# A two-layer hybrid encoder: the first feed-forward block moved into the stage before it, and the edits that go with it

## The chip, the cores and the metric

The program runs on one core of one Trainium2 chip, in one launch. The metric is the device time of an execution in microseconds (us). The engines are TensorE (PE; its weight loads are counted as PEld), VectorE (DVE), ScalarE (ACT), GpSimd (POOL) and SyncE (SP), which here only issues DMAs.

## The reference, cut to what matters

```python
for l in range(2):                      # 1024 prompt + 64 sample tokens, D = 1024
    m = silu(c) @ w_ada[l] + b_ada[l]   # "conditioning": 6 x 1024 numbers for each of 2 sequences
    sh1, sc1, g1, sh2, sc2, g2 = split(m, 6)
    hn = rms_norm(x, norm_mix[l]) * (1 + sc1) + sh1
    o = even_mix(hn) if l == 0 else odd_mix(hn)   # attention + HGRN2 / gated RG-LRU
    x = x + (1 + g1) * o
    hn = rms_norm(x, norm_ffn[l]) * (1 + sc2) + sh2
    x = x + (1 + g2) * ((silu(hn @ ffn_wg[l]) * (hn @ ffn_wu[l])) @ ffn_wd[l])   # D_FF = 2816
y = rms_norm(x, final_norm)
```

All in float32, with products held to about that precision.

## The kernel before, in words

The state x is kept feature by token: eight tiles of 128 partitions by 1088 tokens, of 4.25 KB per partition each. A float32 product is three passes in the faster matmul type: an operand is split into a high part (a cast on ScalarE, L99) and a low part (a subtraction on VectorE or GpSimd, L100), and TensorE adds hi·hi, hi·lo and lo·hi. `load_w` (L105) fetches a weight of 512 KB by one DMA and splits it; `project` (L304) multiplies loaded weights by split operands into the six banks of "t", "z" and "mm", and VectorE adds each result into x (L317).

**Order of the work.** The text fixes what is computed, and a list scheduler with a simulated timeline sets each engine's order; `soon()` and `later()` raise or lower the priority of what is written in them, and DMAs stand in SyncE's queue in the order so found. The wrappers of L60 and L61 (`oPE`, `oV`, `oS`, `oG`, `oD`) keep an instruction behind everything that the text has before it on that engine.

**Before a feed-forward stage.** The last two output projections of the attention stage (`out_group(3)`, L1091) or of the recurrent stage (`odd_out((6, 7))`, L1297) run over four token chunks of 272, in the order of CH4 (L28). After each chunk, `enter`'s `after` (L336) copies the chunk of x to DRAM ("parks" it, eight DMAs), forms its norm, and builds the operands:

```python
rs = norm_stats(CH4[ci], x, stat_tmp)
```

`norm_stats` (L250) squares the eight tiles (six on ScalarE, two on GpSimd), adds them (VectorE, two of the adds on GpSimd), sums over partitions with matmuls against ones (`rms_sum`, L216), takes the power -1/2 on GpSimd (L233) and spreads the roots by matmuls (`rms_spread`, L236). Then come, for each of eight tiles, a VectorE scaling (L351, in place), a ScalarE high part (L352) and a VectorE low part (L353). Each of these has two pieces in the chunk that holds the border between prompt and sample.

**Up stage** (`up_half`, L357). The 22 column blocks of 128 hidden features are worked as 2 "plain" blocks (gate and up product over the four chunks, L416 to L443) and 20 blocks of seven products in Strassen's manner, on four accumulators X, Y, Z, W of two banks each (L498 on). Between plain block 0 and plain block 1, `sums` (L392) turns the scaled x into the operand combinations T1 to T4: VectorE subtracts, T2 and T3 get their low parts there, T1 and T4 on GpSimd:

```python
split(b, T1[k][:, 0, :], T1[k][:, 1, :], G)
split(c, T4[k][:, 0, :], T4[k][:, 1, :], G)
```

The pool of the up stage has these places: wg and wu (raw weights) two each, wh and wl (split weights) six each, two hidden tiles. Phases share SBUF addresses: a tile of a new phase waits for the last use of the tiles that lay there. A block's hidden tile is written to DRAM, as one DMA in a plain block (L442) and as two halves in the others (L481, L487).

**Down stage** (`down_half`, L510). The hidden blocks come back in groups of 2, 3, 3, 3, 3, 3, 3 and 2. `fetch` loads hid (L522) and the down weights, and splits both. `got = fetch(0)` and `unpark` (24 DMAs that bring the parked x back, L505) stand ahead of the first group.

**Conditioning of layer 1.** It is made in layer 0's down stage from 48 rows of 512 KB; an item is a DMA and two passes, both on VectorE, or one of them on GpSimd and ScalarE (`mods_dve`, L189). `ada_tick` (L1115) is called after each chunk of a group and issues up to three items with lowered priority.

## Time and profile before

| | us |
|---|---|
| median of 3 runs (lowest, highest) | 2880.85 (2873.72, 2883.93) |
| the profiled execution | 2879.69 |
| its span, first to last instruction | 2877.9 |

In the span TensorE is busy for 92%, its weight loads for 89%, VectorE 63%, ScalarE 35% and GpSimd 42%. The DMAs move 260.94 MB, 91 GB/s on average. In the lines below, L312 is line 312 of the kernel, `out<-in` are the program's tile names, "x6" counts instructions, and a bracket at the end of a line of a timeline holds the idle time before it and what ended that. "granted clock" or PEclk is the share of TensorE's full clock in a stretch. `SPq` is SyncE's queue of DMA issues.

### The profile page before, as it was taken

The numbers are of one execution on the slowest core, as the hardware profiler recorded it, in microseconds if no ns is written. First come the engines' busy times: TensorE is split into PE (matmuls) and PEld (weight loads), VectorE is DVE, ScalarE is ACT, GpSimd is POOL, SyncE is SP. The second block draws the span as 40 slices with busy tenths as digits, with TensorE's granted clock in tenths as the row PEclk, the third lists the DMA queues.
The fourth block names the chain that finished last, engine by engine and source line by source line (L and its number), as shares of the span: only waits on it lengthen the run. The fifth ranks groups of instructions, "written<-read, shape, count | busy, mean of one in ns | idle before, by whom it ended". The sixth has DMA issues, their size and how long they took to land. (4 is left out here: it accounts for less than half of the span.)

```text
span 2877.9 us, 44436 instructions
## 1 busy us (share of the span) xinstructions
PE 2643.8 (92%) x17680; PEld 2566.8 (89%) x17680; DVE 1813.5 (63%) x2806; ACT 1012.4 (35%) x1839; POOL 1221.1 (42%) x861
## 2 busy tenths in 40 slices
PE   6998999999896999999799959998789999999998
PEld 6898989998786999999799959998789999989997
DVE  8768664568997344444788774658853444446555
ACT  3224343353545222222322255563342222222112
POOL 6446443355635444444344463444344444423222
PEclk9999988999997999999899979999899999999999
DMA  6232112112212222223644411211212222144211
GB/s 234 90 117 82 54 45 83 40 61 106 73 64 79 68 75 80 72 69 135 214 157 169 130 63 56 73 65 54 92 45 83 69 82 76 68 144 154 96 48 63
DMA packets 103984, 260.94 MB, mean 91 GB/s; under 512 B 17120, under 2 KB 42720, under 8 KB 103776
## 3 DMA queue, kind: packets, MB, share of 16 engines
q1 hardware_dynamic: 103776, 258.10, 26.9%
q8 instruction: 139, 2.28, 0.3%
q14 instruction: 69, 0.57, 0.1%
HBM read 207.36 MB, written 50.69 MB: 90 GB/s over the span
## 5 line engine op out<-in xcount | busy, mean ns | idle before, releaser
L100 POOL TENSOR_TENSOR w_lo<-w_raw,w_hi 128x1024 fp32r<-128x1024 f32 x88 | 237.9, 2712 | 382.6 <-ACT w_hi L99 312.2
L100 POOL TENSOR_TENSOR wl<-wg,wh 128x512 fp32r<-128x512 f32 x168 | 220.0, 1311 | 323.3 <-ACT wh L99 316.8
L449 PE MATMUL accW<-op,wh 128*128 128x272 f32 x1280 | 259.1, 290 | 12.4 <-DVE hid L473 7.5
L449 PE MATMUL accZ<-op,wh 128*128 128x272 f32 x1280 | 248.3, 290 | 10.0 <-ACT wh L99 9.9
L449 PE MATMUL accX<-op,wh 128*128 128x272 f32 x1280 | 245.0, 288 | 0.0
L99 ACT CAST wh<-wg 128x512 fp32r<-128x512 f32 x168 | 103.9, 621 | 397.9 <-PE accX L449 114.9
L128 PE MATMUL ps_mm<-h_hi,w_hi 128*128 128x384 f32 (+1 forms) x640 | 219.6, 343 | 11.1 <-ACT w_hi L99 9.7
L449 PEld LDWEIGHTS accW<-op,wh 128*128 128x128 f32 x1280 | 207.8, 191 | 14.2 <-DVE hid L473 6.1
L128 PE MATMUL ps_mm<-h_hi,w_lo 128*128 128x384 f32 (+1 forms) x640 | 217.9, 342 | 1.9 <-POOL w_lo L100 1.9
L128 PE MATMUL ps_mm<-h_lo,w_hi 128*128 128x384 f32 (+1 forms) x640 | 218.2, 341 | 0.0
L449 PEld LDWEIGHTS accZ<-op,wh 128*128 128x128 f32 x1280 | 200.3, 188 | 17.1 <-ACT wh L99 17.1
L449 PEld LDWEIGHTS accX<-op,wh 128*128 128x128 f32 x1280 | 200.4, 188 | 0.5 <-ACT wh L99 0.5
L449 PE MATMUL accX<-op,wl 128*128 128x272 f32 x640 | 187.4, 293 | 1.0 <-POOL wl L100 1.0
L449 PE MATMUL accW<-op,wl 128*128 128x272 f32 x640 | 186.0, 291 | 0.0
L449 PE MATMUL accZ<-op,wl 128*128 128x272 f32 x640 | 184.2, 288 | 0.0
L317 DVE SCALAR_TENSOR_TENSOR x<-ps_mm,mods,x 128x384 f32<-128x384 f32 (+4 forms) x334 | 151.5, 478 | 50.6 <-PE ps_mm L312 50.1
L99 ACT CAST w_hi<-w_raw 128x1024 fp32r<-128x1024 f32 x86 | 88.7, 1049 | 236.5 <-PE ps_mm L312 154.7
L128 PEld LDWEIGHTS ps_mm<-h_hi,w_hi 128*128 128x128 f32 x640 | 126.0, 197 | 14.3 <-ACT w_hi L99 10.5
L467 DVE TENSOR_TENSOR tg<-accY,tg 128x544 f32<-128x544 f32 x40 | 29.0, 724 | 173.1 <-PE accY L449 173.1
L100 POOL TENSOR_TENSOR wl<-wu,wh 128x512 fp32r<-128x512 f32 x88 | 116.5, 1325 | 45.1 <-ACT wh L99 45.1
L317 DVE SCALAR_TENSOR_TENSOR x<-ps_t,mods,x 128x384 f32<-128x384 f32 (+3 forms) x220 | 106.8, 502 | 43.2 <-PE ps_t L312 43.0
L479 DVE TENSOR_TENSOR hid<-accZ,tg 128x544 f32<-128x544 f32 x40 | 29.0, 724 | 166.4 <-PE accZ L449 166.4
(484 smaller groups left out, 8235.7 us busy)
## 6 DMA issues: line engine op xcount, KB each, us to landing
ada_raw<-in_adaT SPq DMA_DIRECT2D x48, 512.0 KB, 3.6
wg<-in_wg SPq DMA_DIRECT2D x44, 512.0 KB, 3.6
wu<-in_wu SPq DMA_DIRECT2D x44, 512.0 KB, 3.6
w_raw<-in_wd SPq DMA_DIRECT2D x44, 512.0 KB, 4.1
hid_dram<-hid SPq DMA_DIRECT2D x80, 272.0 KB, 2.1
hid_lo<-hid_dram SPq DMA_DIRECT2D x40, 544.0 KB, 5.4
w_raw<-in_w_in_even SPq DMA_DIRECT2D x28, 512.0 KB, 3.7
w_raw<-in_adaT SPq DMA_DIRECT2D x24, 512.0 KB, 3.6
```

The source lines that it names most:

```text
L99: S.copy(hi, src)
L100: (lo_eng or G).tensor_sub(lo, src, hi.bitcast(F32))
L128: PE.matmul(ps[:, :n], a[:, k * P:(k + 1) * P], b[:, c0:c0 + n], start=(i == 0), stop=(i == last))
L317: V.scalar_tensor_tensor(x[m][:, r0:r0 + rn], ps[:, r0 - c0:r0 - c0 + rn], gate[:, m, b:b + 1], x[m][:, r0:r0 + rn], ALU.mult, ALU.add)
L449: PE.matmul(acc[:, j, :Q], a[:, k * P:(k + 1) * P], op[k][:, b, c], start=(start == 1 and i == 0), stop=(i == 11), skip_group_check=True)
L467: V.tensor_sub(t, y_, t)
L479: V.tensor_add(hA, z_, t)
```

## The change

The first plain block of each layer leaves the up stage. `first_block` is written in the stage before, behind its last projection, with its weights loaded and split there, and its matmuls and those of the norms of chunks 2 and 3 go through `oPE`: chunk 0's products, then the norm of chunk 2, chunk 1's products, the norm of chunk 3, and the products of chunks 2 and 3. The norm has all its squares on ScalarE and all adds on VectorE. The parked x is one DRAM tensor, brought back by eight DMAs. T1 and T4 get their low parts on VectorE. The conditioning becomes a class: rows of parts 0 to 2 are worked in layer 0's up stage (two per block), parts 3 and 4 in its down stage (one per turn), part 5 in layer 1's up stage. For its two tables "cbc" the up stage has one wu place instead of two and five wh and wl places instead of six. The first two hidden tiles of a down stage are fetched by `prefetch` two blocks before the end of the up stage, into unit tiles; the first down weights and the parked x are loaded through `oD`.

```diff
@@ -105,7 +105,8 @@
     def load_w(src, pool=None, tag="w", raw=None, S=S, lo_eng=None, bufs=2):
         pool = pool or stage["w"]
         raw = raw or raw_tile()
-        dma(raw, src)
+        if src is not None:
+            dma(raw, src)
...
+    def inv_rms(parts, n, scale_, PE=PE):
+        return rms_inv(rms_sum(parts, n, PE), n, scale_, PE=PE)
+    def norm_stats(chunk, x, tmp, PE=PE, pool=(1, 2)):
         c0, n = chunk
...
             S.activation(a, x[2 * e][:, c0:c0 + n], AF.Square)
-            if e in (1, 2):
+            if e in pool:
                 G.tensor_mul(b, x[2 * e + 1][:, c0:c0 + n], x[2 * e + 1][:, c0:c0 + n])
             else:
                 S.activation(b, x[2 * e + 1][:, c0:c0 + n], AF.Square)
             V.tensor_add(a, a, b)
             if e:
-                (G if e in (1, 2) else V).tensor_add(a, a, acc)
+                (G if e in pool else V).tensor_add(a, a, acc)
             acc = a
-        return inv_rms([lambda: acc], n, 1.0 / 1024)
+        return inv_rms([lambda: acc], n, 1.0 / 1024, PE)
 
...
@@ -333,14 +334,14 @@
 
...
-        def after(ci):
+        def chunk(ci, PE=PE):
             c0, n = CH4[ci]
             r = slice(c0, c0 + n)
             if not B:
                 B.extend([halves(u(t, F32R, "op")) for _ in range(4)] for t in (tag, tag, "C", "C"))
             for k in range(KD):
-                dma(x_dram[k][:, r], x[k][:, r])
-            rs = norm_stats(CH4[ci], x, stat_tmp)
+                dma(x_dram[:, k, r], x[k][:, r])
+            rs = norm_stats(CH4[ci], x, stat_tmp, PE, ())
             o = c0 % HT
             for k in range(KD):
...
-        return (B, x), after
-
-    def up_half(l, plain, t_tag, op_tag):
-        (B12, B11, B21, B22), x = plain
+        def after(ci):
+            if ci < 2:
+                chunk(ci)
+
+        return B, chunk, after
+    def plain_chunk(ci, ws, B, hid, gate, up, PE):
+        c0 = CH4[ci][0]
+        c = slice(c0 % HT, c0 % HT + Q)
+        for acc, w2_ in ((gate, ws[:2]), (up, ws[2:])):
+            i = 0
+            for w, op in zip(w2_, ((B[1], B[2]), (B[0], B[3]))[ci % 2]):
+                for k in range(4):
+                    for a, b in ((w[0], 0), (w[0], 1), (w[1], 0)):
+                        PE.matmul(acc, a[:, k * P:(k + 1) * P], op[k][:, b, c], start=(i == 0), stop=(i == 23))
+                        i += 1
+        h = hid[:, c0:c0 + Q]
+        with soon():
+            S.activation(h, gate, AF.Silu)
+            V.tensor_mul(h, h, up)
+    def first_block(l, plain, w_gate, w_up, hid):
+        B, chunk, _ = plain
+        ws = [(hi[:, o:o + 512], lo[:, o:o + 512]) for hi, lo in (w_gate, w_up) for o in (0, 512)]
+        for ci, tag in enumerate(("z", "t", "mm", "z")):
+            plain_chunk(ci, ws, B, hid, bank(tag)[:, :Q], bank(tag)[:, :Q], oPE)
+            if ci < 2:
+                chunk(ci + 2, oPE)
+        dma(hid_dram[0], hid)
+
+    class Ada:
+        def __init__(self, todo):
+            self.todo = [(i, j) for i in todo for j in range(KD)]
+
+        def open(self, pool, raw, junk):
+            self.raw, self.junk = raw, junk
+            self.cb = load_cbc([pool.tile([P, 1024], F32, name="cbc", tag="cbc", bufs=2) for v in range(2)],
+                               junk(F32))
+
+        def some(self, n):
+            with later():
+                for _ in range(min(n, len(self.todo))):
+                    i, j = self.todo.pop(0)
+                    raw = self.raw()
+                    dma(raw, I["adaT"][48 + i * KD + j])
+                    mods_dve(1, i * KD + j, self.cb, raw, lambda: self.junk(BF16), j % 2 == 0)
+                    if j == KD - 1:
+                        finish_mods(1, i)
+
+    def up_half(l, plain, x, t_tag, op_tag, ada, prefetch):
+        B = B12, B11, B21, B22 = plain[0]
         with phase_pool(f"up{l}") as fp:
-            layout(fp, ("t4", NT, 4), ("t1", NT, 4), ("t3", NT, 4), ("wg", 1024, 2), ("wu", 1024, 2), ("s1", 512, 1),
-                   ("wh", 512, 6), ("wl", 512, 6), ("hid0", NT, 2))
+            layout(fp, ("t4", NT, 4), ("t1", NT, 4), ("t3", NT, 4), ("wg", 1024, 2), ("wu", 1024, 1), ("s1", 512, 1),
+                   ("wh", 512, 5), ("wl", 512, 5), ("cbc", 1024, 2), ("hid0", NT, 2))
+            hid0 = lambda: fp.tile([P, NT], F32, name="hid0", tag="hid0", bufs=2)
 
             def w_split(src):
-                hi = fp.tile([P, 512], F32R, name="wh", tag="wh", bufs=6)
-                lo = fp.tile([P, 512], F32R, name="wl", tag="wl", bufs=6)
+                hi = fp.tile([P, 512], F32R, name="wh", tag="wh", bufs=5)
+                lo = fp.tile([P, 512], F32R, name="wl", tag="wl", bufs=5)
...
             def fetch(f):
                 wg = fp.tile([P, 1024], F32, name="wg", tag="wg", bufs=2)
-                wu = fp.tile([P, 1024], F32, name="wu", tag="wu", bufs=2)
+                wu = fp.tile([P, 1024], F32, name="wu", tag="wu", bufs=1)
                 dma(wg, I["wg"][l, f])
                 dma(wu, I["wu"][l, f])
                 return wg[:, :512], wg[:, 512:], wu[:, :512], wu[:, 512:]
...
                     split(d, T3[k][:, 0, :], T3[k][:, 1, :], V)
-                    split(b, T1[k][:, 0, :], T1[k][:, 1, :], G)
-                    split(c, T4[k][:, 0, :], T4[k][:, 1, :], G)
+                    split(b, T1[k][:, 0, :], T1[k][:, 1, :], V)
+                    split(c, T4[k][:, 0, :], T4[k][:, 1, :], V)
...
                 def plain_block(f, order):
-                    hid = fp.tile([P, NT], F32, name="hid0", tag="hid0", bufs=2)
+                    hid = hid0()
                     with soon():
                         ws = [w_split(w) for w in fetch(f)]
                     for n, ci in zip("XYZW", order):
                         acc = new_acc(n)
...
-                        h = hid[:, c0:c0 + Q]
-                        with soon():
-                            S.activation(h, acc[:, 0, :Q], AF.Silu)
-                            V.tensor_mul(h, h, acc[:, 1, :Q])
+                        plain_chunk(ci, ws, B, hid, acc[:, 0, :Q], acc[:, 1, :Q], PE)
                     dma(hid_dram[f], hid)
...
-                plain_block(0, range(4))
                 ops = sums()
                 plain_block(1, (1, 3, 0, 2))
+                if ada:
+                    with later():
+                        ada.open(fp, lambda: hid0()[:, :1024], lambda dt: u(t_tag, dt, "junk")[:, :1024])
                 for f in range(2, FF):
+                    if f == FF - 2:
+                        got = prefetch()
                     X, Y, Z, W = (new_acc(n) for n in "XYZW")
...
+                    if ada and 2 < f < FF - 3:
+                        ada.some(2)
...
+        return got
 
     def unpark(tag):
         x = [u(tag, name="x") for _ in range(KD)]
-        for c0, n in CH:
-            for k in range(KD):
-                dma(x[k][:, c0:c0 + n], x_dram[k][:, c0:c0 + n])
+        for k in range(KD):
+            oD(x[k], x_dram[:, k, :])
         return x
...
-    def down_half(l, fp, x_tag, t_tag, use):
+    def fetch_hid(f, hi, lo):
+        dma(lo.bitcast(F32), hid_dram[f])
+        with soon():
+            split(lo.bitcast(F32), hi, lo, V)
+        return hi, lo
+
+    def hid_units(f, tag):
+        return fetch_hid(f, u(tag, F32R, "hid_hi"), u(tag, F32R, "hid_lo"))
+
+    def down_half(l, fp, x_tag, t_tag, got, use):
         first = [sum(GROUPS[:gi]) for gi in range(len(GROUPS))]
+        last_group = len(GROUPS) - 1
+        w0 = []
+        for f in range(GROUPS[0]):
+            raw = raw_tile()
+            oD(raw, I["wd"][l, f])
+            w0.append(load_w(None, fp, "wd", raw, bufs=6))
+        x = unpark(x_tag)
         def fetch(gi):
             hs, ws = [], []
             for f in range(first[gi], first[gi] + GROUPS[gi]):
-                if gi == len(GROUPS) - 1:
+                if gi == last_group:
                     t = fp.tile([P, 2, NT], F32R, name="hid", tag="hid", bufs=2)
-                    hi, lo = t[:, 0, :], t[:, 1, :]
+                    hs.append(fetch_hid(f, t[:, 0, :], t[:, 1, :]))
                 else:
-                    tag = t_tag if f < 2 or f % 2 else "C"
-                    hi, lo = u(tag, F32R, "hid_hi"), u(tag, F32R, "hid_lo")
-                dma(lo.bitcast(F32), hid_dram[f])
-                with soon():
-                    split(lo.bitcast(F32), hi, lo, V)
-                hs.append((hi, lo))
+                    hs.append(hid_units(f, t_tag if f % 2 else "C"))
                 ws.append(load_w(I["wd"][l, f], fp, "wd", bufs=6))
             return ws, hs
-        got = fetch(0)
-        x = unpark(x_tag)
         tick, after, last = use(x)
         for gi in range(len(GROUPS)):
-            ws, hs = got if gi == 0 else fetch(gi)
-            if gi == len(GROUPS) - 1 and last:
+            ws, hs = fetch(gi) if gi else (w0, got)
...
-    x_dram = [dram.tile([P, NT], F32, name=f"x_dram{k}") for k in range(KD)]
+    x_dram = dram.tile([P, KD, NT], F32, name="x_dram")
...
-        plain, after = enter(0, x, "A", slots(mp, "kv", 3, 2, 4))
-        out_group(3, after, CH4)
+        plain = enter(0, x, "A", slots(mp, "kv", 3, 2, 4))
+        om = lambda nm: mp.tile([P, 1024], F32R, name=nm, tag="om", bufs=2)
+        be = lambda nm: mp.tile([P, 1024], F32R, name=nm, tag="be", bufs=6)
+        w_first = []
+        for wt, hi, lo in (("wg", om, om), ("wu", be, be)):
+            raw = raw_tile()
+            dma(raw, I[wt][0, 0])
+            w_first.append((hi("w_hi"), lo("w_lo")))
+            split(raw, *w_first[-1])
+        out_group(3, plain[2], CH4)
+        first_block(0, plain, *w_first, mp.tile([P, NT], F32, name="hid0", tag="wt", bufs=2))
...
-    up_half(0, plain, "B", "A")
+    first_hid = lambda tag: lambda: [hid_units(f, tag) for f in range(GROUPS[0])]
+    got = up_half(0, plain, x, "B", "A", Ada((0, 1, 2)), first_hid("B"))
...
-                      fp.tile([P, 1024], F32, name="cbs", tag="ada_raw", bufs=2))
-        todo = [(i, j) for i in range(6) for j in range(KD)]
-
...
+        ada = Ada((3, 4))
         box2 = []
 
         def use(x):
             with later():
+                raw = lambda: fp.tile([P, 1024], F32, name="ada_raw", tag="ada_raw", bufs=2)
+                ada.open(fp, raw, lambda dt: raw() if dt == F32 else fp.tile([P, 1024], BF16, name="junk", tag="junk"))
...
-            return ada_tick, after, None
-
...
+            return lambda ci: ada.some(1), after, None
...
-        plain, after = enter(1, x, "B", slots(gp, "un", 12, 2, 4, Q))
+        plain = enter(1, x, "B", slots(gp, "un", 12, 2, 4, Q))
...
-        odd_out((6, 7), "un", after, CH4)
+        w_first = [load_w(I[wt][1, 0]) for wt in ("wg", "wu")]
+        odd_out((6, 7), "un", plain[2], CH4)
+        first_block(1, plain, *w_first, un_("hid0"))
...
-    up_half(1, plain, "A", "B")
+    got = up_half(1, plain, x, "A", "B", Ada((5,)), first_hid("A"))
...
-        down_half(1, fp, "B", "A", lambda x: (None, None, lambda ws, hs: finish(ws, hs, x)))
+        down_half(1, fp, "B", "A", got, lambda x: (None, None, lambda ws, hs: finish(ws, hs, x)))
```

## Rows read from the trace of the kernel before

**Rows 1.** The page's busy times of the engines, with shares and instruction counts.
```profile
PE 2643.8 (92%) x17680; PEld 2566.8 (89%) x17680; DVE 1813.5 (63%) x2806; ACT 1012.4 (35%) x1839; POOL 1221.1 (42%) x861
```

**Rows 2.** TensorE's waits, whole span: us in total, times, longest us.
```profile
PE ps_o L240 <- POOL r L233: 19.1, 9, 4.8
...
PE ps_t L312 <- ACT w_hi L99: 16.1, 3, 10.6
...
PE accX L435 <- POOL wl L100: 12.1, 2, 6.1
PE accX L435 <- ACT wh L99: 10.8, 2, 5.5
PE accZ L449 <- ACT wh L99: 9.9, 30, 0.3
...
PE accW L449 <- DVE hid L473: 7.5, 4, 3.7
...
PE accW L449 <- DVE tg L484: 4.9, 4, 2.4
```

**Rows 3.** Stretches: us, busy PE PEld DVE ACT POOL, PEclk, DMA share, GB/s.
```profile
865.00:883.00 18.00, 7.03 (x32) 6.54 (x31) 15.43 (x39) 7.68 (x18) 8.53 (x7) 0.50 0.44 155
883.00:907.00 24.00, 24.00 (x186) 24.00 (x186) 22.06 (x49) 18.78 (x39) 6.75 (x6) 0.95 0.22 67
907.00:940.00 33.00, 21.49 (x157) 20.94 (x156) 14.72 (x21) 12.60 (x25) 22.60 (x13) 0.84 0.10 34
960.00:1360.00 400.00, 394.44 (x3099) 388.44 (x3098) 182.18 (x201) 110.03 (x184) 168.73 (x131) 1.00 0.24 81
1360.00:1420.00 60.00, 41.78 (x245) 39.81 (x245) 35.98 (x41) 22.04 (x23) 14.92 (x6) 0.83 0.62 226
1420.00:1640.00 220.00, 213.19 (x1268) 209.98 (x1267) 182.19 (x316) 58.45 (x79) 110.13 (x43) 0.99 0.49 160
1640.00:1720.00 80.00, 49.46 (x272) 45.96 (x272) 65.88 (x136) 36.62 (x80) 48.91 (x40) 0.77 0.20 67
```

**Rows 4.** TensorE in order of time before layer 0's first block (start, us, work).
```profile
871.59 1.44 PE L224 MATMUL ps_o<-ones,ntmp 128*128 128x1 f32 x6 [5.44 <-DVE ntmp L262]
...
881.27 1.65 PE L240 MATMUL ps_o<-ident,r 128*128 128x128 f32 x6 [3.56 <-POOL r L233]
```

**Rows 5.** VectorE in order of time around the same block.
```profile
866.39 2.55 DVE L353 SCALAR_TENSOR_TENSOR op<-x,mods,op 128x272 fp32r<-128x272 f32 x6
...
870.28 0.90 DVE L353 SCALAR_TENSOR_TENSOR op<-x,mods,op 128x272 fp32r<-128x272 f32 x2
...
880.02 8.53 DVE L353 SCALAR_TENSOR_TENSOR op<-x,mods,op 128x272 fp32r<-128x272 f32 x8
...
907.10 0.72 DVE L100 TENSOR_TENSOR op<-x,op 128x544 fp32r<-128x544 f32 x1
```

**Rows 6.** GpSimd in order of time behind that block (operand splits).
```profile
906.95 15.07 POOL L100 TENSOR_TENSOR op<-x,op 128x544 fp32r<-128x544 f32 x7 [17.25 <-ACT op L99]
...
923.19 1.34 POOL L100 TENSOR_TENSOR op<-x,op 128x544 fp32r<-128x544 f32 x1
```

**Rows 7.** SyncE's DMA queue ahead of that block.
```profile
836.20 34.51 SPq L342 DMA_DIRECT2D x_dram<-x  x32
```

**Rows 8.** SyncE's DMA queue at both down starts, TensorE at the second.
```profile
1349.04 7.43 SPq L505 DMA_DIRECT2D x<-x_dram  x14
...
2589.42 0.86 SPq L108 DMA_DIRECT2D w_raw<-in_wd  x2
...
2592.33 0.32 SPq L487 DMA_DIRECT2D hid_dram<-hid  x1
...
2595.09 0.54 PE L312 MATMUL ps_t<-hid_hi,w_hi 128*128 128x384 f32 x1 [4.99 <-ACT w_hi L99]
```

**Rows 9.** Conditioning passes (tile junk) behind down stage 0: us, DVE, ACT busy, DMA.
```profile
1640.00:1690.00 50.00, 13.32 (x22) 5.72 (x10) 0.94 0.33 107
```

More of the change, by code (lines that the diff above doesn't have):

```diff
@@ L244, in rms_inv @@
         return rms_spread(rms_pow(ps, n, scale_, V, G), n, PE)
-    def inv_rms(parts, n, scale_):
-        return rms_inv(rms_sum(parts, n), n, scale_)
-    def norm_stats(chunk, x, tmp):
+    def inv_rms(parts, n, scale_, PE=PE):
+        return rms_inv(rms_sum(parts, n, PE), n, scale_, PE=PE)
+    def norm_stats(chunk, x, tmp, PE=PE, pool=(1, 2)):
         c0, n = chunk
@@ L1110, in hybrid_encoder @@
         ntmp = lambda: fp.tile([P, 384], F32, name="ntmp", tag="ntmp", bufs=7)
-        cb = load_cbc([fp.tile([P, 1024], F32, name="cbc", tag="cbc", bufs=2) for v in range(2)],
-                      fp.tile([P, 1024], F32, name="cbs", tag="ada_raw", bufs=2))
-        todo = [(i, j) for i in range(6) for j in range(KD)]
-        def ada_tick(ci):
-            with later():
-                for n in range(3):
-                    if not todo:
-                        return
-                    i, j = todo.pop(0)
-                    raw = fp.tile([P, 1024], F32, name="ada_raw", tag="ada_raw", bufs=2)
-                    dma(raw, I["adaT"][48 + i * KD + j])
-                    mods_dve(1, i * KD + j, cb, raw,
-                             lambda: fp.tile([P, 1024], BF16, name="junk", tag="junk"), j % 3 != 0)
-                    if j == KD - 1:
-                        finish_mods(1, i)
+        ada = Ada((3, 4))
         box2 = []
@@ L1134, in use @@
             box2.append(box)
-            return ada_tick, after, None
-        x = down_half(0, fp, "A", "B", use)
-        assert not todo
+            return lambda ci: ada.some(1), after, None
+        x = down_half(0, fp, "A", "B", got, use)
+        assert not ada.todo
     h = box2[0][0]
```

15 lines of the change are left out of this document (2 added, 13 removed).

## The prediction

> **What bounds the kernel now.** I read the busy times first, then what TensorE waits for, then the stretches between stages, and last the queues of the other engines around those stretches. TensorE is busy for 2643.8 of 2877.9 us [rows 1], so the other 234 us are the most that any edit outside its own work can win. The list of its waits [rows 2] puts the large ones at the seams: the inverse roots of the norm (19.1 us in nine), the weights of the plain block (12.1 and 10.8 us, two waits each, one per layer), the first down weights (16.1 us, the longest 10.6). The table of stretches [rows 3] gives the size of each: TensorE is busy for 7.0 of the 18 us before the first block, 21.5 of 33 after it, 41.8 of 60 at the first down start, 213.2 of 220 in that down stage and 49.5 of 80 in the norm behind it. Layer 1 repeats layer 0's seam with the same waits (the pairs of [rows 2]).
>
> **First block inside the preceding stage.** Today TensorE ends the output projection at 866.2 (871.6 less 5.4 of idle), waits for the sums of chunk 2, its roots, and the roots of chunk 3, and begins the block at about 882.6, when the last spread is through [rows 4]. The stretch from 883 to 907 is its four chunks [rows 3], 24 us without a gap, 6 each. The change puts chunk 0 at once behind the projection. But the kept order then reads: chunk 0, sum and spread for chunk 2, chunk 1, sum and spread for chunk 3, chunk 2, chunk 3; nothing can slip between a sum and its spread, which lie some 2 us apart because of the power on GpSimd (19.1 us in nine waits [rows 2]). VectorE decides the rest. It finishes chunk 1's operands at 871.2 [rows 5] and is busy for 15.4 of the 18 us of that stretch [rows 3]; eight adds of the statistics now come to it from GpSimd, 0.43 us each by the 272-column operations there (2.55 us for six), 3.4 us. So: chunk 0 from 866.2 to 872.2; sum at 875.0, spread out at 879.8; chunk 1 to 885.8; sum, 2 us, spread out at 890.6; chunk 2 to 896.6. Chunk 3's operands need 32 short VectorE operations, about 0.27 us each for 272 columns in two pieces (half of 0.43, with some overhead), 8 us behind the spread that frees them, so until about 898; the gate half of chunk 3 ends there, the up half 3 us later, some 902. Today it ends at 907: gain 4.5 us. Ends: without any wait 4 x 6 us end at 890, gain 17; with chunks 0 and 1 at the half clock that rows show after today's gap (granted clock 0.50 in that stretch [rows 3]) they take 12 us more, a loss of 5 to 7. One more thing helps: chunk 2's eight operand passes took 8.53 us while GpSimd split the first weights, against 2.55 for six elsewhere [rows 5]; these splits are now done before.
>
> **The weights of block 1.** Their wait, 5.4 and 6.05 us per layer [rows 2], has two causes in the queues. The loads stood behind 32 parked x copies on the DMA queue, until 870.7 [rows 7], and the last two weights' low parts stood behind seven operand splits on GpSimd, 15.07 us [rows 6]. Both go: T1 and T4 split on VectorE costs it 8 x 0.72 = 5.8 us per layer [rows 5], and all four weights of block 1 find free slots since block 0 keeps its own elsewhere. In layer 0 something new is late: by the tile widths in the code the wg buffers of the up stage lie on the two "wt" slots, and the block's hid0 is now in one of them. A wg load then waits for the last chunk's product and its write, which I estimate at 3 us, and from issue to first use a weight takes 5.7 us at the second down start [rows 8]: some 8.7 us in all. The up halves of block 1, 12 us, can cover that if they are issued first. I take 4 us uncovered (ends 0 and 11.4), so a gain of 7.5 in layer 0; in layer 1, where the hidden tile is in "un" and the buffers are free, 10. Both seams together: 2 x 4.5 + 7.5 + 10 = 26.5 us.
>
> A rule of the Trainium skill speaks against splitting on VectorE: SBUF — State Buffer, section "Who interferes with whom", says that a VectorE instruction with two SBUF inputs and a GpSimd one that reads SBUF exclude each other, and the second waits for the whole of the first. The rows agree in one direction: a split on GpSimd beside the sums took 15.07 / 7 = 2.15 us, alone 1.34 [rows 6], while VectorE's stayed at 0.72 [rows 5]; in the other they show it too, chunk 2's passes at 1.07. By the rule block 1's four low parts take 0.8 us more each beside the longer sums, 3.4 us if uncovered, and the seams' sum would be some 23 instead of 26.5.
>
> **Conditioning in three stages.** Of 48 items 16 stay in down stage 0, one per turn instead of three; 24 go to up stage 0 (two per block), 8 to up stage 1. An item costs VectorE one or two passes, and a pass 1.21 us (13.32 us for eleven, each with its accumulator read [rows 9]). These eleven still run between 1640 and 1690, where it has 65.9 of 80 us to do and TensorE idles 30.5 [rows 3], and they make the evictions late before it (6.8 us idle in the down stage). With a third of the work at a third of the pace they end in time. I take 5 of 6.8 and 7 of 13.3: 12 us (ends 0 and 20). In the up stages 36 and 12 passes, 58 us of VectorE, lie beside products; it is busy there for 182 of 400 us [rows 3]. They cost nothing while the accumulators are read in time; if each pass stood in front of one such read, 58 us. The DMA waits of these passes hold VectorE's queue, with the accumulators' readers behind them. I take 4.
>
> **Down stage.** Today the first down weights are issued at 2589.4, before the last hidden half is written at 2592.3, and TensorE starts at 2595.1, 5.7 after the issue [rows 8]. The new loads are kept behind everything on SP's queue that the text has before them, the last hidden write included: issue 2592.7, start 2598.4. That is 8.3 us after the last product (2590.1) where layer 1 now waits 5.0; layer 0 waits 10.6 since the cast stands behind other work, and gains 2.2. Net a loss of 1.1. The eight x loads (4.46 MB) now follow those weights, where today they are issued 30 us early [rows 8]; at the 226 GB/s seen at 0.62 busy [rows 3] all arrive 20 us later or sooner, about when TensorE has filled its six banks and gone round; I take 2 us per layer (ends 0 and 10). What leaves VectorE's queue are the first two hidden splits, in front of the reads of W in the last block, which cost 7.5 + 4.9 us [rows 2]; I take back 4. Sum: a loss of 1.
>
> **Rings.** wh and wl get five slots instead of six, wu one buffer instead of two. Today each block waits 0.33 us for a cast (9.9 in 30 [rows 2]). The next wu can be loaded only after the last split of the present one. Ends: the 9.9 gone, or 1.5 us per block; I take nothing, nearest to that row.
>
> **Sum.** -26.5 - 12 + 4 + 1 = -33.5 from the profiled execution's own 2879.7 (span 2877.9, 1.8 outside it): 2846. The median shown, 2880.85, is 1.2 higher; I say 2847.
>
> **Rivals.**
> Seams held by VectorE: the same operand passes in the same queue, chunk 3 no earlier, layer 0's weights late by all 8.7 us. For it: VectorE busy 15.4 of 18 there. Against: 5 us of collision gone. Only 5 to 10 us of the 26.5 remain: 2866.
> Down start: the pinned loads delay x by 10 us per layer and nothing comes back in the last block: 16 + 4 more, 2867. For it: the x loads stand early today without any cost; against: six banks of slack.
> Slower: the ring of five. In the block loop a product's weight must be released, cast and split before its next use; with one slot fewer each block waits once more, a cast and a split, 0.6 + 1.3 us less the present slack of some 0.4: 1.5 us in each of 40 blocks, 60 us: 2906. From 0.85 us per block on it eats the whole gain. For it: each block already waits for a cast; against: TensorE's order is chosen with the ring known.
> More gain: weights covered wholly, the norm gaining all 20, the last block's waits gone: 2826.
> That the change does not do what it says: the order is kept only on TensorE; if VectorE's queue puts chunk 2's statistics late, chunk 1 waits too; that is the first rival's time.
>
> **How the numbers follow.** Forecast 0.47 (own range 2834 to 2862), VectorE's seams 0.18, down start 0.13, the ring 0.15, more gain 0.07. The range 2824 to 2888 leaves out the ring at full price and the tail of the last case. A measurement of this kernel tells 0.3%, 8.6 us, from nothing. Faster: 0.46 + 0.13 + 0.05 + 0.07 = 0.71; same: 0.01 + 0.04 + 0.06 = 0.11; slower: 0.15 + 0.01 + 0.02 = 0.18.
>
> **What would show it.** Right: the idle before the first block gone and instead two gaps of 2 us or more between sum and spread among its chunks; block 1's wait under 4 us; no conditioning pass in the last down group; first down product some 8 us after the last up product in both layers. Wrong: TensorE idle per block above 0.33 us in the block loop, waits for hid or x at the down start above 5 us, or chunk 2 and 3 starting when they do today.

## The result: slower by 1.1%

The changed kernel takes 2913.3 us (median of 4; 2908.7 to 2917.6) against 2881.7 for the kernel before, a ratio of 1.0114 with a 95% interval of 1.0089 to 1.014. The forecast was 2847, with a range of 2824 to 2888. The profiled executions are 2908.7 us (span 2906.9) and 2879.7 (2877.9).

The page's busy times after:

```profile
PE 2653.2 (91%) x17680; PEld 2570.7 (88%) x17680; DVE 1860.4 (64%) x2854; ACT 1018.5 (35%) x1847; POOL 1206.3 (41%) x803
```

TensorE does the same 17680 matmuls; its idle time grew from 234 us [rows 1] to 254, and its busy time by 9. Where the 29 us of span lie is seen by cutting both spans at the same points, read from the first and last matmuls of each stage. "18 blocks" are the last 18 of the 20 seven-product blocks.

| stretch, us | before | after | difference |
|---|---|---|---|
| start to the end of the attention stage's projection | 866.2 | 865.0 | -1.2 |
| to the 18 blocks, layer 0 (both plain blocks, sums) | 121.3 | 118.7 | -2.6 |
| 18 blocks, layer 0 | 400.9 | 447.9 | +47.0 |
| down stage 0 and norm, to the recurrent stage's first product | 327.6 | 305.5 | -22.1 |
| recurrent stage, to its projection's end | 353.1 | 346.7 | -6.4 |
| to the 18 blocks, layer 1 | 121.4 | 123.3 | +1.9 |
| 18 blocks, layer 1 | 399.6 | 412.3 | +12.7 |
| rest | 287.8 | 287.6 | -0.2 |

The loss is in the two up stages, 59.7 us. TensorE's waits over the span (us in total, times, longest), to be held against [rows 2]:

```profile
PE accW L487 <- DVE hid L515: 34.3, 16, 2.3
PE accX L370 <- ACT wh L99: 25.4, 2, 12.8
...
PE accX L487 <- ACT wh L99: 11.9, 30, 0.7
...
PE ps_t L313 <- ACT w_hi L99: 10.5, 3, 5.0
...
PE accX L370 <- POOL wl L100: 9.0, 2, 5.6
```

The first line has grown from 7.5 us in 4 waits [rows 2]: now the products on W waited 16 times for VectorE's read of W (L515, L473 before). Fourteen of these waits, of 2.32 us each, stand among the 16 blocks with conditioning (12 blocks in layer 0, 4 in layer 1); the other two, of 0.91 us, stand in the last block of each layer. From one block's first product on Y to the next one's it takes 25.1 to 27.3 us with conditioning and 22.0 without (21.8 before). The second line says that the wait for block 1's weights did not go; it doubled.

One block with conditioning on VectorE, in order of time (start, us, work):

```profile
1012.97 0.72 DVE L512 TENSOR_TENSOR hid<-accZ,tg 128x544 f32<-128x544 f32 x1 [3.11 <-PE accZ L487]
1013.61 2.34 DVE L196 SCALAR_TENSOR_TENSOR junk<-hid,cbc 128x1024 bf16<-128x1024 f32 x1
...
1015.88 0.71 DVE L526 TENSOR_TENSOR tg<-accW,tg 128x544 f32<-128x544 f32 x1
1016.51 1.13 DVE L441 SCALAR_TENSOR_TENSOR wg<-wg 128x512 f32<-128x512 f32 x1
1017.57 2.92 DVE L528 TENSOR_TENSOR hid<-hid,tg 128x544 f32<-128x544 f32 x1
1020.41 2.31 DVE L196 SCALAR_TENSOR_TENSOR junk<-hid,cbc 128x1024 bf16<-128x1024 f32 x1
...
1022.66 2.30 DVE L196 SCALAR_TENSOR_TENSOR junk<-hid,cbc 128x1024 bf16<-128x1024 f32 x1
...
1025.49 0.71 DVE L515 TENSOR_TENSOR hid<-accW,hid 128x544 f32<-128x544 f32 x1
...
1035.77 0.72 DVE L509 TENSOR_TENSOR tg<-accY,tg 128x544 f32<-128x544 f32 x1 [6.78 <-PE accY L487]
```

and on GpSimd and TensorE in the same block:

```profile
1014.83 2.27 POOL L100 TENSOR_TENSOR wl<-wu,wh 128x512 fp32r<-128x512 f32 x1
1017.06 2.85 POOL L193 TENSOR_TENSOR hid<-hid,cbc 128x1024 f32<-128x1024 f32 x1
1019.87 4.01 POOL L100 TENSOR_TENSOR wl<-wg,wh 128x512 fp32r<-128x512 f32 x2
```

```profile
1026.26 0.52 PE L487 MATMUL accW<-op,wh 128*128 128x272 f32 x2 [2.32 <-DVE hid L515]
```

Three passes of the conditioning and an operation that lasts 2.92 instead of 0.72 us stand between VectorE's read of Z and its read of W. A little later VectorE is idle for 6.8 us. TensorE loses 2.32 us, and then runs slowly. Two stretches of TensorE (columns as in [rows 3]), just behind this wait and after it:

```profile
1026.20:1030.20 4.00, 3.94 (x19) 3.94 (x20) 2.65 (x5) 0.62 (x1) 1.75 (x1) 0.58 0.44 154
1030.20:1040.00 9.80, 9.60 (x77) 9.38 (x75) 1.14 (x2) 2.24 (x4) 2.58 (x2) 1.00 0.05 18
```

A granted clock of 0.58 for 4.0 us (near the lower of the two levels, 1.2 of 2.4 GHz) costs 1.7 us more. Wait and clock together are 4.0 us here; the mean loss over the 16 blocks is 59.7 / 16 = 3.7. The clock did not fall each time: it fell behind ten of the fourteen waits, and in layer 0 a block with such a fall mostly takes 26.6 us and one without 25.1. By these numbers the fourteen waits (32.5 us) and ten falls (some 17) explain about 50 of the 59.7 us; the other 10 were not followed line by line.

The seam in layer 0 (a seam is the stretch from the projection's end to the 18 blocks), TensorE and SyncE's queue; instructions that go through the wrappers carry the wrappers' line, L51:

```profile
873.53 0.94 PE L51 MATMUL ps_o<-ident,r 128*128 128x128 f32 x6 [1.32 <-POOL r L234]
882.57 0.93 PE L51 MATMUL ps_o<-ident,r 128*128 128x128 f32 x6 [1.49 <-POOL r L234]
...
909.60 0.82 PE L370 MATMUL accX<-op,wh 128*128 128x272 f32 x2 [12.61 <-ACT wh L99]
915.15 0.59 PE L370 MATMUL accX<-op,wl 128*128 128x272 f32 x1 [3.36 <-POOL wl L100]
```

```profile
901.93 0.32 SPq L386 DMA_DIRECT2D hid_dram<-hid  x1
904.75 0.33 SPq L425 DMA_DIRECT2D wg<-in_wg  x1
```

The first block runs as meant, right behind the projection, and ends at 897.0 instead of 907.9. Block 1 then waits 12.6 us for the casts of its weights and 3.4 for a low part: their loads were issued at 904.75, behind the write of the first block's hidden tile. In layer 1 the waits are 12.8 and 5.6 us; there the loads follow the write at once (issued at 2125.72), and the casts of these weights, at 2131.20, come right behind the sums' casts on ScalarE. The wait for a low part has a third cause, in VectorE and GpSimd:

```profile
906.27 7.70 DVE L100 TENSOR_TENSOR op<-x,op 128x544 fp32r<-128x544 f32 x12
```

```profile
909.63 6.70 POOL L100 TENSOR_TENSOR wl<-wg,wh 128x512 fp32r<-128x512 f32 x2 [27.12 <-ACT wh L99]
```

The first of these two low parts took 5.46 us, the second 1.28. The first ended 1.1 us behind the last of VectorE's twelve splits in a row (913.97), of which eight are those of T1 and T4 that the change had moved there. In layer 1 it took 7.73 us.

### The profile page after: what moved, and what is told of

Its sections match the earlier page's. It is cut to its first block, busy times and chain, and to the rows that moved or that the text cites. A ratio compares the mean times of both kernels' runs of the same rounds, so it can differ in the third digit from the quotient of the medians.

```text
span 2906.9 us, 44480 instructions
## 1 busy us (share of the span) xinstructions
PE 2653.2 (91%) x17680; PEld 2570.7 (88%) x17680; DVE 1860.4 (64%) x2854; ACT 1018.5 (35%) x1847; POOL 1206.3 (41%) x803
## 5 line engine op out<-in xcount | busy, mean ns | idle before, releaser
L100 POOL TENSOR_TENSOR wl<-wg,wh 128x512 fp32r<-128x512 f32 x164 | 259.1, 1581 | 365.8 <-ACT wh L99 365.3
L487 PE MATMUL accW<-op,wh 128*128 128x272 f32 x1280 | 266.1, 294 | 41.5 <-DVE hid L515 34.3
L487 PE MATMUL accX<-op,wh 128*128 128x272 f32 x1280 | 257.2, 297 | 13.2 <-ACT wh L99 11.9
L487 PEld LDWEIGHTS accX<-op,wh 128*128 128x128 f32 x1280 | 208.1, 196 | 20.6 <-ACT wh L99 19.2
L100 POOL TENSOR_TENSOR wl<-wu,wh 128x512 fp32r<-128x512 f32 x84 | 125.2, 1491 | 107.7 <-ACT wh L99 107.7
L487 PEld LDWEIGHTS accX<-op,wl 128*128 128x128 f32 x640 | 125.7, 196 | 7.5 <-POOL wl L100 7.5
```

The lines of the kernel that those rows point to most:

```text
L100: (lo_eng or G).tensor_sub(lo, src, hi.bitcast(F32))
L487: PE.matmul(acc[:, j, :Q], a[:, k * P:(k + 1) * P], op[k][:, b, c], start=(start == 1 and i == 0), stop=(i == 11), skip_group_check=True)
```

## The experiments

Times are medians beside runs of the kernel before on the same chip; its medians there were 2878.3 (e1_back to e4_before_cond), 2879.7 (n1_vonly, s1_gq, s3_first, s4_t_pool) and 2881.4 (p1_placed_pool, b1_before_placed, s5_more). Between these groups the ratios compare better than the times.

| run | us | ratio to before (95%) | 18 blocks, layers 0 and 1 | down 0 and norm | seams, layers 0 and 1 |
|---|---|---|---|---|---|
| e1_back | 2870.8 | 0.998 (0.997 to 0.999) | 401.2, 399.7 | 326.0 | 120.7, 120.7 |
| e2_back_rings | 2876.8 | 1.000 (0.999 to 1.001) | 403.5, 400.3 | 329.1 | 118.2, 118.2 |
| e3_placed | 2852.8 | 0.992 (0.990 to 0.994) | 399.8, 399.6 | 307.4 | 118.1, 121.8 |
| e4_before_cond | 2915.6 | 1.014 (1.012 to 1.016) | 448.8, 412.3 | 301.7 | 125.3, 122.4 |
| n1_vonly | 2883.5 | 1.002 (1.001 to 1.003) | 420.7, 405.6 | 309.7 | 118.1, 123.2 |
| p1_placed_pool | 2852.7 | 0.990 (0.989 to 0.992) | 395.4, 397.7 | 309.1 | 119.2, 122.1 |
| b1_before_placed | 2862.0 | 0.994 (0.992 to 0.995) | 404.0, 400.1 | 299.8 | 124.4, 121.6 |
| s1_gq | 2856.7 | 0.993 (0.991 to 0.994) | 399.6, 401.2 | 306.2 | 118.5, 123.2 |
| s3_first | 2835.8 | 0.985 (0.983 to 0.987) | 400.6, 398.8 | 306.2 | 110.7, 112.7 |
| s4_t_pool | 2839.1 | 0.986 (0.984 to 0.988) | 401.2, 400.3 | 305.7 | 111.1, 111.0 |
| s5_more | 2829.6 | 0.982 (0.981 to 0.984) | 400.5, 398.7 | 301.4 | 106.9, 112.8 |

The stretches are from one profiled execution each. The first stretch (863 to 871 us among them) shows that a stretch of one execution can't be read closer than a few us.

### Is it the conditioning or the ring? (e1_back, e2_back_rings, e4_before_cond)

```diff
-    got = up_half(0, plain, x, "B", "A", Ada((0, 1, 2)), first_hid("B"))
+    got = up_half(0, plain, x, "B", "A", None, first_hid("B"))
-        ada = Ada((3, 4))
+        ada = Ada(range(6))
-            return lambda ci: ada.some(1), after, None
+            return lambda ci: ada.some(3), after, None
-    got = up_half(1, plain, x, "A", "B", Ada((5,)), first_hid("A"))
+    got = up_half(1, plain, x, "A", "B", None, first_hid("A"))
```

> The changed kernel with all 48 conditioning items back in down stage 0, three per turn; the rest, the ring of five included, as changed. Theory (the passes in the up stages stand in front of the reads of accumulator W): the 16 blocks that take 26.3 us instead of 22.0 lose 4.3 each, 69 us; the down stage takes back some 16 of the 22 us that it had gained: 2913 - 69 + 16 = 2860. Rival (the ring of five slots and the single wu buffer make the blocks slow): the blocks stay at 26, and the down stage gets slower: 2929.

Measured 2870.8, 43 us below the change: the blocks are back at 22.0 us (401.2 and 399.7 in the table), the down stage is back at 326. The theory was 11 us too low, partly since the blocks gave back 59.3 us instead of 69 and the down stage gave up 20.5 instead of 16: nearly all that it had gained was conditioning. With the conditioning back, the rest of the change is worth 7.5 us against the kernel before.

The second run has that and in addition the rings of before in the up stage:

```diff
-                   ("t3", NT, 4), ("wg", 1024, 2), ("wu", 1024, 1), ("s1", 512, 1),
-                   ("wh", 512, 5), ("wl", 512, 5), ("cbc", 1024, 2), ("hid0", NT, 2))
+                   ("t3", NT, 4), ("wg", 1024, 2), ("wu", 1024, 2), ("s1", 512, 1),
+                   ("wh", 512, 6), ("wl", 512, 6), ("hid0", NT, 2))
```

> As the run before it, and six wh and wl slots and two wu buffers as before the change. Theory: blocks without conditioning take 22.0 us with five slots and 21.8 with six, 0.2 to 0.25 in 40 blocks, 8 to 10 us: 2860 - 9 = 2851. Rival (the ring is the main cost): 60 to 70 us below the run before it.

Measured 2876.8, 6 us slower and not 9 faster. With six places a block takes 21.8 us instead of 22.0, but the last blocks take it back (28.1 and 25.6 us). Five places cost nothing; the rival of the prediction with the price of 60 us is refuted.

The third takes the kernel before and gives it the class, the two items per block and the small ring alone (class Ada and the layout line are those of the changed kernel):

```diff
+                if ada:
+                    with later():
+                        ada.open(fp, lambda: hid0()[:, :1024], lambda dt: u(t_tag, dt, "junk")[:, :1024])
...
+                    if ada and 2 < f < FF - 3:
+                        ada.some(2)
...
-    up_half(0, plain, "B", "A")
+    up_half(0, plain, "B", "A", Ada((0, 1, 2)))
...
+        ada = Ada((3, 4))
...
-            return ada_tick, after, None
+            return lambda ci: ada.some(1), after, None
...
-    up_half(1, plain, "A", "B")
+    up_half(1, plain, "A", "B", Ada((5,)))
```

> The kernel before with the conditioning in three stages alone, in the changed kernel's way (two items per block in the up stages, ring of five and one wu buffer with it). Theory: 16 blocks lose 4.3 us, 40 blocks 0.25 by the ring, down stage 0 gains 16: 2882 + 69 + 10 - 16 = 2945, slower than the whole change. Rival (the loss is an interaction with the moved first block or the late weights of block 1): no slower than 2882.

Measured 2915.6, as slow as the whole change. The loss needs no other part of it. My 2945 was too high for three reasons: the blocks lost 60.6 us instead of 69, the ring's 10 us don't exist, and down stage 0 gained 26 instead of 16.

### Place in the queue, or sharing with GpSimd? (e3_placed, n1_vonly, p1_placed_pool)

```diff
+        def work(self):
+            for (i, j), raw in self.got:
+                for v in range(2):
+                    oV.scalar_tensor_tensor(self.junk(BF16), raw, 1.0, self.cb[v], ALU.mult, ALU.mult,
+                                            accum_out=mods[1][:, i * KD + j, v:v + 1])
...
                         with soon():
                             use()
+                        if ada and use is p4 and 3 < f:
+                            ada.work()
...
-                        ada.some(2)
+                        ada.load(2)
```

> The changed kernel, with the same items in the same up stages, two per block, but all four passes of a block on VectorE (none on GpSimd and ScalarE), kept in program order right behind the last product's read of Z in the block, where VectorE idles 6.8 us, and their rows loaded a block earlier. Theory (place in the queue decides, not the load): four passes of 1.22 us fit into 6.8 us, no read of W waits, the blocks go to about 22: 2913 - 69 = 2844; if each pass takes 2.3 us there, 9.2 us against 6.8 idle, the next read of Y waits up to 2.4 us less the slack and half of the loss stays: 2880. Rival (the load of the passes or the sharing with GpSimd costs the time wherever they stand): 2913.

Measured 2852.8, 60 us below the change: as many items in as many blocks, one more pass per block on VectorE, and no loss. Tile junk on VectorE in the two kernels' layer 0, changed first, then placed (min, median, max ns):

```profile
L196 DVE SCALAR_TENSOR_TENSOR junk<-hid,cbc x36: 2297/2314/2915, 965.7 to 1257.8; 128x1024 bf16<-128x1024 f32 x36
```

```profile
L51 DVE SCALAR_TENSOR_TENSOR junk<-hid,cbc x48: 1210/1216/2318, 999.5 to 1244.5; 128x1024 bf16<-128x1024 f32 x48
```

At the new place the median pass takes 1.22 us instead of 2.31. The read of W now stands ahead of the passes and waits for TensorE, and not the other way round:

```profile
1013.42 0.72 DVE L532 TENSOR_TENSOR hid<-accW,hid 128x544 f32<-128x544 f32 x1 [0.36 <-PE accW L504]
...
1020.40 2.31 DVE L51 SCALAR_TENSOR_TENSOR junk<-hid,cbc 128x1024 bf16<-128x1024 f32 x1
...
1027.17 0.71 DVE L526 TENSOR_TENSOR tg<-accY,tg 128x544 f32<-128x544 f32 x1
```

That the rows are loaded a block earlier is not the reason: in the changed kernel no pass of the up stages waited for the DMA of its row. TensorE runs through at full clock (two blocks of the placed version):

```profile
1012.00:1056.00 44.00, 43.22 (x339) 42.34 (x338) 30.73 (x39) 11.88 (x20) 21.06 (x14) 1.00 0.37 122
```

The next run leaves the place to the scheduler and takes GpSimd and ScalarE out of the conditioning:

```diff
-                    mods_dve(1, i * KD + j, self.cb, raw, lambda: self.junk(BF16), j % 2 == 0)
+                    mods_dve(1, i * KD + j, self.cb, raw, lambda: self.junk(BF16), False)
```

> The changed kernel with all passes of the up stages on VectorE and none on GpSimd and ScalarE; their place in VectorE's queue is left to the scheduler, as in the changed kernel, and four of them stand in front of the read of W in each of 16 blocks. Theory (place in the queue): the blocks stay at 25 to 28 us, and the time at 2900 to 2925. Rival (GpSimd's multiplication, 2.85 us, which one VectorE operation waited for, is the cause): the blocks go to 22, 2845.

Measured 2883.5, outside both: it loses 26 us in the 36 blocks (420.7 - 400.9 and 405.6 - 399.6) instead of 60. I had taken GpSimd's part for a detail. But the edit changed more than that: the scheduler set the orders anew, TensorE's too, and the blocks with conditioning now go in turn 19.4 and 26.8 to 28.4 us instead of 25.1 to 27.3 each. How much of the 34 us is the sharing with GpSimd and how much the new order, this run does not show.

The third run has the placed passes and again GpSimd's multiplication, in every second item:

```diff
                 for v in range(2):
+                    if v and j % 2 == 0:
+                        G.tensor_mul(raw, raw, self.cb[v])
+                        S.activation(self.junk(BF16), raw, AF.Identity, accum_out=mods[1][:, i * KD + j, v:v + 1])
+                        continue
```

> The version with the placed passes (2853), but every second item has one of its two passes on GpSimd and ScalarE again, as in the changed kernel; three passes stay on VectorE at the place behind the read of Z. The version with all passes on VectorE at the scheduler's place (2884) had shown that GpSimd's multiplication has part in the loss. Theory (the multiplication hurts only where VectorE operations that W's read waits for stand beside it): the blocks stay at 22.0 us, 2853 within 5. Rival (GpSimd's 2.85 us per block hold up its own low parts, or VectorE's, wherever they stand): 1 to 2 us more in each of 16 blocks, 2870 to 2885.

Measured 2852.7. At this place the same multiplication costs nothing:

```profile
1026.38 3.31 POOL L411 TENSOR_TENSOR hid<-hid,cbc 128x1024 f32<-128x1024 f32 x1 [1.17 <-DVE junk L51]
```

```profile
1027.37 3.41 DVE L51 SCALAR_TENSOR_TENSOR junk<-hid,cbc 128x1024 bf16<-128x1024 f32 x1
...
1031.42 0.72 DVE L530 TENSOR_TENSOR tg<-accY,tg 128x544 f32<-128x544 f32 x1 [0.63 <-ACT tg L527]
```

It stretches a pass to 3.41 us, and VectorE is still early for the next read, of Y; TensorE's waits for reads of W in layer 0 are 0.9 and 3.7 us, as in e3_placed (0.9 and 3.8). So the place decides whether the passes cost anything. That sharing raises the price of a bad place is argued from durations (0.72 to 2.92 us, 1.21 to 2.31) and not isolated: TensorE's order here is again another one, the scheduler's, and its blocks take 21.3 to 22.3 us. Before the change VectorE's low-part splits had shown the same sharing [rows 5, 6]. The Trainium skill, SBUF — State Buffer, section "Who interferes with whom", has a VectorE operation with two SBUF inputs wait for the whole of a GpSimd one that reads SBUF and began first; the trace agrees: L528 began 0.51 us behind the multiplication of 2.85 us, took 2.92 and ended 0.58 us behind it. The prediction weighed that rule for the splits only.

### Where did the seams' gain go? (b1_before_placed, s1_gq, s3_first, s4_t_pool)

The first of these is e4_before_cond with the diff of e3_placed on top, so the kernel before with only the conditioning moved and the small ring.

```diff
+                        if ada and use is p4 and 3 < f:
+                            ada.work()
...
-                        ada.some(2)
+                        ada.load(2)
```

> The kernel before with nothing changed but the conditioning in three stages, with placed passes on VectorE (so the first block in the up stage, T1 and T4 split on GpSimd, the old down start). Theory (the moved first block, the splits on VectorE and the down start together bring only 2 to 5 us in the changed kernel, since the wait for block 1's weights stayed): 2853 + 4 = 2857. Rival (they bring what was forecast, 28 us, and something else lost it): 2881.

Measured 2862.0. Against e3_placed (2852.8), the moved first block, the splits on VectorE and the down start together are worth 9 us by the times and 5 by the ratios, whose intervals overlap, where the prediction had 26.5 - 1 = 25.5 for them and the expectation above 28.

```diff
-        dma(hid_dram[0], hid)
+        nc.gpsimd.dma_start(hid_dram[0], hid)
...
-                   ("t3", NT, 4), ("wg", 1024, 2), ("wu", 1024, 1), ("s1", 512, 1),
-                   ("wh", 512, 5), ("wl", 512, 5), ("cbc", 1024, 2), ("hid0", NT, 2))
+                   ("t3", NT, 4), ("hid0", NT, 2), ("wg", 1024, 2), ("wu", 1024, 1),
+                   ("s1", 512, 1), ("wh", 512, 5), ("wl", 512, 5), ("cbc", 1024, 2))
```

> The version with the placed passes (2853), and the block 0 hidden tile written to DRAM by GpSimd's queue instead of SyncE's; in the up stage the places of wg and wu lie where the norm's temporaries were and not on that hidden tile, so that the loads of block 1 follow the parked x at once. The casts of these weights still stand behind the twelve casts of T1, T3 and T4 in ScalarE's order, which end 1.8 us before the first of them in layer 0 and just before it in layer 1. Theory (two causes in a row: the DMA queue, then ScalarE's order): only some 2 us of the two waits of 12.6 and 12.8 us go: 2851. Rival (the hidden write in front of the loads is the whole wait): 25 us go, 2828.

Measured 2856.7: not even the 2 us of the theory came. The loads are now issued 29 us earlier, at 875.75, and TensorE waits all the same:

```profile
875.75 0.33 SPq L442 DMA_DIRECT2D wg<-in_wg  x1
```

```profile
911.72 0.82 PE L370 MATMUL accX<-op,wh 128*128 128x272 f32 x2 [11.61 <-ACT wh L99]
919.40 0.59 PE L370 MATMUL accX<-op,wl 128*128 128x272 f32 x1 [5.50 <-POOL wl L100]
```

The data lie there for some 29 us, while ScalarE first does the sums' bias additions and the casts of T1, T3 and T4, and casts block 1's weights at 911.05:

```profile
893.25 9.29 ACT L467 ACTIVATE x<-x,mods 128x64 f32<-128x64 f32 x15
...
908.86 2.29 ACT L99 CAST op<-x 128x544 fp32r<-128x544 f32 x4 [0.81 <-DVE x L475]
911.05 1.14 ACT L99 CAST wh<-wg 128x512 fp32r<-128x512 f32 x2
```

The next run puts these casts first.

```diff
+                with soon():
+                    ws1 = [w_split(w, oS) for w in fetch(1)]
                 ops = sums()
-                plain_block(1, (1, 3, 0, 2))
+                plain_block(1, (1, 3, 0, 2), ws1)
...
-                        S.activation(v, v, AF.Identity, bias=mods[l][:, 3 * KD + k, b:b + 1])
+                        oS.activation(v, v, AF.Identity, bias=mods[l][:, 3 * KD + k, b:b + 1])
```

> As the run before it, and the weights of block 1 are fetched and split ahead of the sums in the text; the sums' 16 bias additions are kept behind these casts, which are kept behind the last activation of block 0 on ScalarE. Theory: block 1 starts within 2 us behind block 0 and the waits of 12.6 + 3.4 us in layer 0 and 12.8 + 5.6 in layer 1 go; the operands T1 to T4 get ready some 5 us later than now, still inside block 1's 24 us: 2853 - 30 = 2823. Rival (VectorE's sums set the start of the first seven-product block, so that the wait only moves behind block 1): less than 10 us gained, 2845.

Measured 2835.8, 17 us below e3_placed; the seams fall to 110.7 and 112.7 us. In layer 0 block 1 follows within 0.7 us:

```profile
902.59 0.49 PE L370 MATMUL accX<-op,wh 128*128 128x272 f32 x2 [0.69 <-ACT x L51]
904.88 0.40 PE L370 MATMUL accX<-op,wl 128*128 128x272 f32 x1 [1.04 <-POOL wl L100]
```

The other half of the 30 us did not come: the sums now end later, and the first seven-product blocks wait for a low part, 2.0 us in layer 0 and 4.5 in layer 1, and for VectorE, 1.9 and 0.9. Besides, in this one execution layer 0's first block took 34.6 us at a granted clock of 0.84, in that of e3_placed 32.1 at 0.92. Rival and theory each had half.

The next one takes the splits of T1 and T4 back to GpSimd.

```diff
-    split(b, T1[k][:, 0, :], T1[k][:, 1, :], V)
+    split(b, T1[k][:, 0, :], T1[k][:, 1, :], G)
...
-    split(c, T4[k][:, 0, :], T4[k][:, 1, :], V)
+    split(c, T4[k][:, 0, :], T4[k][:, 1, :], G)
```

> As the run before it, with the low parts of T1 and T4 on GpSimd, as before the change. VectorE loses 8 x 0.72 = 5.8 us of work there, GpSimd gets 8 x 1.3 to 2.15 = 10 to 17 us behind block 1's four low parts. Theory (with block 1's weights out of the way, where T1 and T4 are split makes no difference): within 3 us of the run before it. Rival (GpSimd is too slow for them and the first seven-product block waits for T4): 5 to 10 us slower.

Measured 2839.1. Its interval overlaps that of s3_first: with the weights out of the way, the engine of these splits makes no difference that is clear of the noise. In the profiled executions the stretch from the first block's end to the 18 blocks is 3.0 us longer in layer 0 and 1.6 in layer 1.

### A version that beats both (s5_more)

```diff
-    got = up_half(0, plain, x, "B", "A", Ada((0, 1, 2)), first_hid("B"))
+    got = up_half(0, plain, x, "B", "A", Ada((0, 1, 2, 3)), first_hid("B"))
-        ada = Ada((3, 4))
+        ada = Ada((4,))
```

> The best version so far (placed passes, weights of block 1 first, 2836) with 32 instead of 24 items in layer 0's up stage, two in each of 16 blocks, and 8 instead of 16 in the down stage. Theory: the up stage stays at 22.0 us per block; the down stage lost 20 us for 32 items more, so 8 less give back up to 5: 2831 to 2836. Rival (VectorE is no longer late in the down stage with 16 items): no difference, 2836.

Measured 2829.6, 1.8% faster than the kernel before. The blocks stay at 22.0 us and the down stage goes from 306.2 to 301.4.

## Why the prediction was wrong, point by point

**The conditioning in the up stages is the step that failed:** the term taken at 4 us. The prediction put it so: "They cost nothing while the accumulators are read in time; if each pass stood in front of one such read, 58 us. [...] I take 4." It measured 59.7. The mechanism was named, with its bound, and I priced it near zero on VectorE's busy share, 182 of 400 us [rows 3]. A mean share says nothing of the place: the engine idles 6.8 us in the same block, a few us too late. Nothing in the code pins these passes: "lowered priority" leaves their place to an order found on a simulated timeline, so the value should have been near the bound. That the bound, 58, comes out so near 59.7 is luck all the same. It counts 48 passes of 1.21 us; the run shows fourteen waits of 2.32 us, behind passes of 2.31 us and one operation held up by GpSimd, and a lower clock behind ten of them. The DMA waits that the prediction feared in VectorE's queue did not occur in the up stages. And no rival held this case: the forecast's slower ending was the ring, another mechanism.

**Block 1's weights: wrong.** Forecast a gain of 17.5 us; measured a loss, the waits growing from 11.5 us in each layer to 16.0 and 18.4. The two causes that I read [rows 6, 7] did go, and two new ones took their place, both in queues: the first block's hidden write ahead of the loads, and the sums' work ahead of the casts. For layer 0 I had 8.7 us from the last product to the first use, 3 of them for the last chunk's product and its write, and took 4 as exposed and the rest as hidden behind the up halves of block 1. The 3 us stood on no row; from the last product (897.0) to the loads (904.75) it was 7.8, since chunk 3's activation itself stood behind the sums' additions on ScalarE (897.0 to 899.3), and the casts were late besides. The up halves hid nothing, as their loads stood behind the others (L426 at 905.17). For layer 1 I had left almost no wait. And the low parts, which the prediction had at 0.8 us more each and left out of its sum, took 4.2 us (layer 0) and 6.5 us (layer 1) more for the first of them alone, held behind a whole row of VectorE's splits. That T1 and T4 lengthen this row is read from the trace; no run moved them alone while the weights still came late.

**The first block: right in its mechanism, too small in layer 0.** Forecast a gain of 4.5 us per layer; measured from the projection's end to the block's end 9.7 in layer 0 (41.7 to 32.0) and 5.2 in layer 1 (40.5 to 35.3). The granted clock was 0.92 and 0.85 there. The half clock that I feared, 0.50 in [rows 3], belongs to a stretch with the gap in it; the block behind that gap ran at 0.95. The two gaps between sum and spread were 1.3 and 1.5 us in layer 0, not 2. Behind the block the seam grew by 7.1 us in each layer, so 2.6 us of the gain are left in layer 0 and 1.9 are lost in layer 1.

**Down stage 0 and its norm.** Forecast -12 for the conditioning, +1 for the rest; measured -22.1. e1_back shows that nearly all is conditioning (326.0 with it back). The last pass of this stage begins 132 us behind the up stage's end (1563.3), where it was 288 us before (1676.5), so none is left in the last group, as forecast.

**The down start: wrong in its reason.** I had the first down weights behind the last hidden write. They were issued before it (second down start):

```profile
2618.69 0.86 SPq L51 DMA_DIRECT2D w_raw<-in_wd  x2
...
2622.08 0.32 SPq L529 DMA_DIRECT2D hid_dram<-hid  x1
```

TensorE waited 5.0 and 4.9 us, where I had 8.3 twice. So what I said of the order-keeping wrapper was wrong, for DMAs at least; what it does instead was not tried. Layer 0's wait went from 10.6 to 5.0 us, and either edit alone does that: e1_back has the new start and the conditioning back in the down stage and waits 5.1 us; e4_before_cond and b1_before_placed keep the old start and wait 5.1 and 5.0. Beside the moved conditioning the new start thus won nothing there: with the old one the down stage and norm took 301.7 and 299.8 us, with the new one 305.5 and 307.4 (the changed kernel and e3_placed).

**The ring: right** to be taken at nothing (e1_back against e2_back_rings).

**The sum.** The conditioning in the up stages is off by 56 us, the seams by some 26 (-26.5 forecast, -2.6 + 1.9 measured), and the down stage and the recurrent stage gave 10 and 6 more than I had. Why the recurrent stage got shorter was not followed up.

## What to carry to other kernels

Work that is to hide on a partly idle engine costs by its place in that engine's queue, not by the engine's busy share: find the reads that release the busy engine's buffers, and pin the new work behind them. When a wait is removed, look through every queue in front of the same data (DMA, cast, low part): the next one may be just as late, as here with three in a row.

## What was not expected of the hardware

A conditioning pass on VectorE took 1.21 us alone and 2.31 beside GpSimd's splits of 1.3 to 2.3 us each, and 3.41 beside a GpSimd multiplication of 3.31. A TensorE wait of 2.3 us was followed by about 4 us at a granted clock of 0.58, so that wait cost nearly twice its length; it was so behind ten of fourteen. And a low part on GpSimd, 1.28 us alone, took 5.46 and 7.73 us beside an unbroken row of VectorE's splits, which kept their 0.64 us each.
